# A hybrid attention and convolution layer: one signed difference block for pattern 1, and x scaled before its transposes

## The chip, the core and the metric

The kernel runs on one core of a Trainium2 chip. The metric is the device time of one execution in microseconds (us). Within a core TensorE (PE) does matmuls and transposes, VectorE (DVE), ScalarE (ACT) and GpSimd (POOL) work on elements, and SyncE (SP) issues most DMA transfers. Each engine runs its instructions in the order in which they were issued to it; what passes between engines waits on semaphores. Matmuls write into PSUM, eight banks of 128 x 512 floats; all other operands lie in SBUF.

## The reference

One layer on x of 2048 tokens by 1024 columns: a normalisation, one input projection, two groups of mixers, one output projection, a second normalisation, and the residual. There are 12 heads of 64 columns and 256 convolution columns.

```python
h = rmsnorm(x, norm_pre_g)
z = einsum('bsd,de->bse', h, w_in)                    # 1024 -> 4096 columns
q, k, v, g_attn, c_h, c_b, c_c, g_conv = split(z)
q, k = rope(q, pos), rope(k, pos)
for window, dilation in ((128, 1), (512, 4), (2048, 16)):
    # query i sees keys i, i - dilation, ..., i - window, by softmax
    o_i, lse_i = dilated_window_attn(q, k, v, window, dilation)
mix_w = softmax(stack(lses), axis=0)
o = sum(mix_w[..., None] * stack(outs), axis=0)
attn_out = o * silu(g_attn)
conv_out = c_b * causal_depthwise_conv(c_c * c_h, conv_w) * silu(g_conv)
y = einsum('bse,ed->bsd', concatenate([attn_out, conv_out]), w_out)
x = x + rmsnorm(y, norm_post_g)
```

A key at distance 128 from its query belongs to all three patterns. Mixing the three outputs by the softmax of their log-sums is the same as one softmax in which a key counts as often as patterns hold it.

## The kernel before

**Number format.** Every float operand of a product is split into a high part (rounded to fp32r) and a low part (the rest), and a product is three matmuls: high by high, high by low, low by high. ScalarE writes most high parts, VectorE most low parts, by a subtraction that reads the high part.

**Tiling.** The tokens are four chunks b of 512. The 4096 columns are eight groups; groups 0 and 7 are convolution (`conv_unit`), 1 to 6 are pairs of heads (`attn_unit`, index p). So there are 32 steps n = 4 * group + b, 24 of them attention units. A step projects a chunk onto its group's 512 columns: 4 column blocks x 8 pieces kt of 128 rows of x x 3 = 96 matmuls of 512 columns (L961 to L963).

**The first chunks.** `x_chunk(b)` loads four tiles of 128 tokens, transposes them by 128-column pieces kt (TensorE, L504), scales each transposed piece by the weights g of the normalisation while splitting it (ScalarE L511 the high part, VectorE L513 the low part), and stores it to `xt_d` in DRAM, from which the groups 1 to 7 read it again. Beside this it squares the rows (L519), finds the factors 1/RMS (`rsqrt_mean`, twelve small VectorE operations, L429 to L435), and TensorE spreads them over partitions (L526), so that they can multiply the columns: the table t holds cosine, sine (both times the factor) and the factor. Products of q and k are scaled with the rotation, V, the gate and the convolution by the third part of the table (L546, L635).

**One attention unit.** Scores (TensorE, L711 for the patterns of dilation 4 and 16, which are handled together as kind 4, L739 for pattern 1) go to PSUM with 64 rows in use; VectorE adds a mask and takes the row's extreme (L718, L746), ScalarE makes the exponentials P (L722, L750). A key that kind 4 holds twice has ln 2 in its mask. In pattern 1 each block of 128 queries has two blocks of keys, the previous one and its own; P of a query block is 128 x 256. `parts` transposes up to four 128 x 128 blocks of P into one bank (L779), ScalarE copies the high parts (L784) and VectorE takes the low parts (L785) into a tile `pt` (three of them), and `times` multiplies them by V: 256 columns, high and low side by side (L811); where one key block serves two query blocks of pattern 1, one matmul of 512 columns does both (L801). V holds its own high and low parts in 64 columns each, so that the result's bank has four quarters, of which three are wanted. `gather` joins them for each half of 256 queries: ScalarE copies two quarters into two tiles a and t (L827, L828), VectorE adds the third to a (L829), and GpSimd adds a and t (L869). The weights of the two kinds come from their sums (L885 to L909) by way of DRAM, multiply the two results (L918, L919), and GpSimd adds them and applies the gate (L920, L921).

**Output.** When all 32 steps are done, the output projection runs in a form with seven products in place of eight (L1129 to L1131); `finish` and `store` square its rows, take 1/RMS (`rsqrt_root`, L440 to L443), add the residual (L1164) and store (L1166).

**What sets the order.** No order is written out. Each operation is recorded by `add` with an engine, an estimated duration, a priority and what it reads and writes. `Plan.shift` adds the entries of the table SHIFT to the priorities (key: a hundred of priorities and a place in the code). `Plan.schedule` plays a list scheduler over the recorded operations with the program's own cost functions (`actt`, `dvet`, `poolt`, `mmt`, `dmat`) and takes the first ready operation by priority for a free engine; `mode` 1 marks score matmuls (going in or out costs 0.22 in the plan) and `mode` 2 transposes; `port=True` says that VectorE and GpSimd are not planned at once. Banks (`st`, eight of them) and buffers are rings that the plan hands out. `emit` then issues the instructions in the order of the planned starts. So any change of an estimate, or of the operations, moves others.

## Time and profile before

| | |
|---|---|
| median of 3 runs | 1181.58 us (1181.55 to 1181.8) |
| the profiled execution, its own time | 1181.31 us |
| its span in the trace | 1179.3 us |
| mean granted TensorE clock | 0.998 of full speed |
| first and last start of the transposes of P (L779) | 144.2 and 966.0 us |
| VectorE's largest group, L785 | 115.8 us of 180 instructions |
| bytes moved | 280.44 MB, mean 238 GB/s |

The span is shorter than the execution's time by 2.0 us, which lie before its first and behind its last instruction. A group's row in the profile gives the line, the engine, the operation, out <- in by the program's names, the count, busy us, mean ns of one, and the idle time of the engine just before these instructions with what ended it. In a timeline row the first two numbers are start and length in us. Ends of matmuls are modelled, and neighbours overlap in the records.

### The profile page before, as it was taken

Reading aid. Unit: us, or ns where it says so; the run is one execution under the profiler, and the core shown is the slowest. Engines: PE = TensorE matmul, PEld = TensorE weight load, DVE = VectorE, ACT = ScalarE, POOL = GpSimd, SP = SyncE. Lnnn points to the kernel's source line nnn. Section 1 sums busy time; section 2 is a strip of 40 time slices with the busy share of each in tenths; the row PEclk is TensorE's granted clock in tenths of the full one; section 3 lists DMA queues with packets and bytes.
Section 4 is the critical chain, followed back from the end, with each engine's and each line's share of the span. In section 5 each row is a group of like instructions: output and inputs, shape, how many; then the busy total and the mean of one; then the engine's idle time right before and its main releaser. Section 6 shows DMA issues by size and latency. Waiting matters only on the chain.

```text
span 1179.3 us, 20614 instructions
## 1 busy us (share of the span) xinstructions
PE 1167.9 (99%) x6620; PEld 980.1 (83%) x6620; DVE 932.6 (79%) x2331; ACT 707.2 (60%) x1875; POOL 268.5 (23%) x212
## 2 busy tenths in 40 slices
PE   8999999999999999999999999999999999999997
PEld 7888888888888888888888888888888788888886
DVE  4566467886778977897888968898888889788886
ACT  6452356776666776675677658666766653454443
POOL 0001122323223233223332322233322313100000
PEclk9999999999999999999999999999999999999999
DMA  9989867777688856788677676677766878645452
GB/s 333 365 341 349 273 226 234 233 213 240 180 253 264 267 185 206 213 280 272 218 235 237 208 238 219 226 263 252 238 187 215 324 247 334 202 141 189 138 182 89
DMA packets 175292, 280.44 MB, mean 238 GB/s; under 512 B 53712, under 2 KB 109776, under 8 KB 175184
## 3 DMA queue, kind: packets, MB, share of 16 engines
q1 hardware_dynamic: 174896, 278.86, 71.7%
q8 instruction: 52, 0.85, 0.3%
q14 instruction: 56, 0.46, 0.1%
q10 hardware_dynamic: 288, 0.27, 0.1%
HBM read 215.42 MB, written 51.05 MB: 226 GB/s over the span
## 4 chain that ended last, share of the span: by engine, by line
PE 93%; DVE 3%; DMA 2%; ACT 1%; issue 0%; SPq 0%; DVEq 0%; ACTq 0%
PE st L961 19%; PE st L963 19%; PE st L962 19%; PE st L779 6%; PE st L811 6%; PE st L1131 4%; PE st L1130 4%; PE st L1129 4%; PE st L711 4%; PE st L739 3%; PE st L801 2%; PE st L504 1%; PE st L675 1%; DMA xt<-xt 1%; DMA g<-in_w_in 0%; DMA p<-in_x 0%
## 5 line engine op out<-in xcount | busy, mean ns | idle before, releaser
L961 PE MATMUL st<-xt,w 128*128 128x512 f32 x1024 | 414.3, 405 | 0.0
L963 PE MATMUL st<-xt,w 128*128 128x512 f32 x1024 | 400.8, 391 | 0.7 <-DVE w L471 0.7
L962 PE MATMUL st<-xt,w 128*128 128x512 f32 x1024 | 399.7, 390 | 0.1
L963 PEld LDWEIGHTS st<-xt,w 128*128 128x128 f32 x1024 | 192.2, 188 | 43.9 <-DVE w L471 1.5
L961 PEld LDWEIGHTS st<-xt,w 128*128 128x128 f32 x1024 | 192.5, 188 | 40.8 <-issue 5.9
L962 PEld LDWEIGHTS st<-xt,w 128*128 128x128 f32 x1024 | 193.0, 188 | 33.1 <-DVE xt L513 0.4
L722 ACT ACTIVATE p<-p,sm 128x128 f32<-128x128 f32 (+3 forms) x192 | 105.8, 553 | 73.6 <-DVE sm L718 73.5
L785 DVE TENSOR_TENSOR pt<-st,pt 128x512 fp32r<-128x512 f32 (+1 forms) x180 | 115.8, 675 | 24.0 <-ACT pt L784 22.7
L827 ACT COPY uu<-st 64x256 f32<-64x256 f32 x192 | 69.6, 366 | 94.2 <-PE st L811 86.4
L829 DVE TENSOR_TENSOR uu<-st,uu 64x256 f32<-64x256 f32 x192 | 78.8, 419 | 57.8 <-ACT uu L828 49.4
L718 DVE CUSTOM_DVE_ANT_0 p<-st,cst 128x128 f32<-128x128 f32 (+3 forms) x192 | 82.0, 486 | 40.8 <-PE st L711 40.4
L811 PE MATMUL st<-pt,v 128*128 128x256 f32 x660 | 111.7, 284 | 0.2 <-DVE pt L785 0.2
L811 PEld LDWEIGHTS st<-pt,v 128*128 128x128 f32 x660 | 98.9, 189 | 9.4 <-DVE pt L785 0.9
L869 POOL TENSOR_TENSOR uu<-uu 128x512 f32<-128x512 f32 x48 | 69.5, 1449 | 155.1 <-DVE uu L829 113.4
L784 ACT CAST pt<-st 128x512 fp32r<-128x512 f32 (+1 forms) x180 | 96.7, 579 | 8.9 <-PE st L779 7.8
L750 ACT ACTIVATE p<-p,e 128x256 f32<-128x256 f32 (+1 forms) x192 | 94.4, 496 | 3.4 <-DVE e L746 3.3
L779 PE MATMUL st<-cst,p 128*128 128x128 f32 x708 | 95.1, 273 | 0.0
L779 PEld LDWEIGHTS st<-cst,p 128*128 128x128 f32 x708 | 82.2, 140 | 11.0 <-issue 0.9
L920 POOL TENSOR_TENSOR uu<-uu 128x512 f32<-128x512 f32 x24 | 37.3, 1556 | 170.1 <-DVE uu L919 170.1
L828 ACT COPY uu<-st 64x256 f32<-64x256 f32 x192 | 68.5, 367 | 10.6 <-POOL uu L921 5.6
L643 POOL TENSOR_TENSOR rp<-rp,cs 128x512 f32<-128x512 f32 x24 | 37.8, 1573 | 142.4 <-DMA rp<-rp 115.7
L746 DVE CUSTOM_DVE_ANT_0 p<-st,cst 128x256 f32<-128x256 f32 (+1 forms) x192 | 66.7, 411 | 3.5 <-PE st L739 3.4
(240 smaller groups left out, 1885.4 us busy)
## 6 DMA issues: line engine op xcount, KB each, us to landing
xt<-xt SPq DMA_DIRECT2D x256, 512.0 KB
cs<-t SPq DMA_DIRECT2D x28, 768.0 KB
raw<-in_w_in SPq DMA_DIRECT2D x58, 256.0 KB
rp<-rp SPq DMA_DIRECT2D x192, 64.0 KB
vd<-v SPq DMA_DIRECT2D x24, 512.0 KB
v<-vd SPq DMA_DIRECT2D x96, 128.0 KB
ab<-ad SPq DMA_DIRECT2D x48, 256.0 KB
uu<-mix SPq DMA_DIRECT2D x27, 256.0 KB
```

The costliest lines, as they stand in the source:

```text
L718: add("DVE", dvet(w) + 0.01, pr + URG, lambda h=h, r=r, P4=P4: vec.tensor_tensor_reduce(P4.ap[:, r, 0:w], ps[h].ap[:, (r - r0) * w:(r - r0 ...
L722: add("ACT", actt(w) + 0.19, pr, lambda h=h, r=r, P4=P4: act.activation(P4.ap[:, r, 0:w], P4.ap[:, r, 0:w], AF.Exp, bias=s4(0, h)[:, r:r + ...
L750: add("ACT", actt(256 - lo[g]) + 0.19, pr, lambda h=h, g=g, P1=P1: act.activation(P1.ap[:, g, lo[g]:], P1.ap[:, g, lo[g]:], AF.Exp, bias=E ...
L779: nc.tensor.transpose(ps.ap[:, i * 128:(i + 1) * 128], pp.ap[:, a, c * 128:(c + 1) * 128], ident)
L784: add("ACT", actt(m * 128, True), pr + URG, lambda: act.copy(pt.ap[:, :m, 0, :], p4()), r=[ps], w=[(pt, 0)])
L785: add("DVE", dvet(m * 128), pr + URG, lambda: vec.tensor_tensor(pt.ap[:, :m, 1, :], p4(), f(pt.ap[:, :m, 0, :]), op=ALU.subtract), r=[ps, ...
L811: mm(dst, v, pt.ap[:, i], start=s, stop=e, skip_group_check=kind == 1)
L827: add("ACT", actt(256, True) + HALF / 2, pr + URG, lambda: act.copy(cols(a, lo), o()[hi:hi + 64, 0]), r=[O], w=[(a, (h, half))])
L829: add("DVE", dvet(256), pr + URG, lambda: vec.tensor_tensor(cols(a, lo), o()[lo:lo + 64, 0], cols(a, lo), op=ALU.add), r=[O], w=[(a, (h, h ...
L961: mm(z.ap, w.ap[:, 0, js], xt.ap[:, 0], start=kt == 0, stop=False)
L962: mm(z.ap, w.ap[:, 0, js], xt.ap[:, 1], start=False, stop=False)
L963: mm(z.ap, w.ap[:, 1, js], xt.ap[:, 0], start=False, stop=kt == KT - 1)
```

## The change

**Pattern 1.** The mask of the previous block now keeps only keys nearer than 128, so that of the two blocks of a query block, previous and own, at most one has an entry at each place. The key at distance 128 is counted three times in kind 4 instead (ln 3 in its mask). `square` subtracts the previous block from the own one in SBUF (VectorE, L859) and transposes the difference: four transposes into one bank per head (L866). The positive part is the own block, the negative part the previous one. ScalarE takes each by a Relu with scale 1 or -1 (L873), VectorE the low parts by a max or min with 0 and a subtraction or addition (L880, L876), with the sign turned, so that `gather` subtracts where it added. No matmul of 512 columns is left in PV (L898).

**Joining.** ScalarE copies one quarter (L914); VectorE adds the second and adds or subtracts the third (L919, L917). The tile t and GpSimd's addition go.

**x.** For chunks 1 to 3 the rows are squared early, and x is multiplied in place by the factors (ScalarE rows 0 and 2, L541; VectorE rows 1 and 3, L538) before it is transposed (L552). For these chunks nothing is spread over partitions, the table holds cosine and sine alone and is read from the input, the gate's tanh reads PSUM directly (L591, L592), and V and the convolution's columns are copied by ScalarE (L700, L638, L596). Chunk 0 is scaled by its table as before (L570, earlier L526).

**Start and end.** The first loads of x and weights go out earlier and by two queues; the first tile of x is transposed into two banks, one scaled by ScalarE and one by VectorE (`first_tile`); the 12 matmuls of its piece run as four high by high, four high by low, four low by high; the warm-up has 7 products, not 8, and two later ones go. `rsqrt_root` has one operation less on the chain, and the last output tile is stored in two halves, the second through ScalarE's queue.

**The plan.** Some estimates change (GpSimd's constant 0.25 to 0.07, those of the weights' small operations, the cost of going into transposes 0.07 to 0.02), and the table SHIFT has other entries throughout.

```diff
-    prev1 = np.where(tk >= tq, zero, no)
+    prev1 = np.where(tk > tq, zero, no)
...
-    prev4 = np.where(four, np.where(k >= q, twice, zero), near)
-    diag4 = np.where(k <= q, np.where(four, twice, zero), no)
+    thrice = np.float32(-np.log(3.0))
+    prev4 = np.where(four, np.where(k >= q, np.where(k - q == 96, thrice, twice), zero), near)
+    diag4 = np.where(k <= q, np.where(four, np.where(q - k == 32, thrice, twice), zero), no)
...
 SHIFT = {
-    (-1, 41): 100, (0, 15): 90, (1, 8): 3, (1, 41): 120, (4, 63): 90, (4, 72): 60, (4, 76): 240, (5, 64): 203,
+    (-2, 27): -10, (0, 13): -123, (0, 29): -90, (1, 13): 260, (1, 14): -220, (1, 16): -150, (1, 45): 120,
...
-                        o.dur += 0.07
+                        o.dur += 0.02
...
-    return n * 0.00239 + 0.25
+    return n * 0.00239 + 0.07
...
-        vec.tensor_scalar(t, t, -0.5, 1.5, op0=ALU.mult, op1=ALU.add)
-        vec.tensor_tensor(y, y, t, op=ALU.mult)
+        vec.scalar_tensor_tensor(y, t, 1.5, y, op0=ALU.add, op1=ALU.mult)
...
+        if b:
+            factors(b * 100 - 150)
+            for i, z in enumerate(xn):
+                if i % 2:
+                    x_last.append(add("DVE", dvet(D), b * 100 - 140, lambda i=i, z=z: vec.tensor_scalar(
+                        z.ap, z.ap, root.ap[:, 8 + i:9 + i], None, op0=ALU.mult), r=[root], w=[(z, h) for h in range(5)], port=True))
+                else:
+                    x_last.append(add("ACT", actt(D, ptr=True), b * 100 - 140, lambda i=i, z=z: act.activation(
+                        z.ap, z.ap, AF.Copy, scale=root.ap[:, 8 + i:9 + i]), r=[root], w=[(z, h) for h in range(5)]))
...
+        def square(h):
+            pp, ps, first = P[h, 1], Tok(st_r), int(b == 0)
+            add("DVE", dvet(C), pr, lambda: vec.tensor_tensor(
+                pp.ap[:, first:, 128:], pp.ap[:, first:, 128:], pp.ap[:, first:, 0:128], op=ALU.subtract),
...
+                for g in range(4):
+                    nc.tensor.transpose(ps.ap[:, g * 128:(g + 1) * 128], pp.ap[:, g, 128:], ident)
...
+            for s, pt in enumerate(two):
+                lo = first if not s else 0
+                add("ACT", actt((4 - lo) * 128, True), pr + URG, lambda pt=pt, lo=lo, s=s: act.activation(
+                    pt.ap[:, lo:, 0, :], p4(lo), AF.Relu, scale=1.0 if s else -1.0), r=[ps], w=[(pt, 0)])
+                if s:
+                    add("DVE", dvet(C), pr + URG, lambda pt=pt: vec.scalar_tensor_tensor(
+                        pt.ap[:, :, 1, :], p4(0), 0.0, f(pt.ap[:, :, 0, :]), op0=ALU.max, op1=ALU.subtract, reverse1=True),
...
-            add("ACT", actt(256, True) + HALF / 2, pr + URG, lambda: act.copy(cols(t, lo), o()[lo:lo + 64, 1]), r=[O], w=[(t, (h, half))])
...
+            for l in range(2):
+                if l and kind == 1:
+                    fn = lambda: vec.tensor_tensor(cols(a, lo), cols(a, lo), o()[lo:lo + 64, 1], op=ALU.subtract)
+                else:
+                    fn = lambda l=l: vec.tensor_tensor(cols(a, lo), o()[lo:lo + 64, l], cols(a, lo), op=ALU.add)
...
-                    add("POOL", poolt(C), pr, lambda a=a, t=t: pool.tensor_tensor(a.ap, a.ap, t.ap, op=ALU.add), r=[t], w=[a], port=True)
...
-    add("PE", 3.4, -1e6, lambda: warm_up(8), w=[warm])
+    add("PE", 3.0, -1e6, lambda: warm_up(7), w=[warm])
```

Three places show what the new plan does with it. In the rows below out <- in are the program's names with the number of the buffer, then the shape.

The first is TensorE in the first stage, where chunk 0's projections end (L961 to L963 before, L1062 to L1064 after), its factors are spread (L526, L570) and chunk 1's transposes begin (L504, L552). Before:

```order
L961 MATMUL st_117<-xt_127,w_136 128x512
L962 MATMUL st_117<-xt_127,w_136 128x512
L963 MATMUL st_117<-xt_127,w_136 128x512
L526 MATMUL st_115<-cst,sm_161 128x128 x4
L961 MATMUL st_118<-xt_127,w_136 128x512
L962 MATMUL st_118<-xt_127,w_136 128x512
L963 MATMUL st_118<-xt_127,w_136 128x512
```

After:

```order
L1062 MATMUL st_117<-xt_126,w_135 128x512
L1063 MATMUL st_117<-xt_126,w_135 128x512
L1064 MATMUL st_117<-xt_126,w_135 128x512
L570 MATMUL st_112<-cst,sm_158 128x128 x4
L552 MATMUL st_118<-cst,p_185 128x128
L552 MATMUL st_118<-cst,p_186 128x128
L552 MATMUL st_118<-cst,uu 128x128 x2
L552 MATMUL st_111<-cst,p_185 128x128
L552 MATMUL st_111<-cst,p_186 128x128
```

Before, 63 of the step's 96 matmuls stood ahead of the spread, 33 behind it, and chunk 1's transposes began 21 matmuls later. Now all 96 stand ahead of it, and the transposes of chunk 1's eight pieces follow in a row.

The second is TensorE in the middle of an attention unit, at pattern 1 of one head. Before, the end of one head's PV (L801, L811) and the transposes of the next blocks:

```order
L811 MATMUL st_117<-pt_193,v_179 128x2x128
L801 MATMUL st_117<-pt_193,v_177 128x2x2x128
L811 MATMUL st_117<-pt_193,v_177 128x2x128
L779 MATMUL st_116<-cst,p_188 128x128 x4
L779 MATMUL st_114<-cst,p_189 128x128 x4
L779 MATMUL st_115<-cst,p_189 128x128 x4
L961 MATMUL st_119<-xt_126,w_133 128x512
L962 MATMUL st_119<-xt_126,w_133 128x512
```

After, at one head's square (L866):

```order
L898 MATMUL st_114<-pt_188,v_174 128x2x128
L898 MATMUL st_114<-pt_189,v_174 128x2x128
L1062 MATMUL st_116<-xt_123,w_132 128x512
L1063 MATMUL st_116<-xt_123,w_132 128x512
L1064 MATMUL st_116<-xt_123,w_132 128x512
L866 MATMUL st_113<-cst,p_186 128x128 x4
L1062 MATMUL st_112<-xt_124,w_133 128x512
L1063 MATMUL st_112<-xt_124,w_133 128x512
L1064 MATMUL st_112<-xt_124,w_133 128x512
```

Groups of four transposes, two of them for each head, have become one; 18 projection matmuls stand between this one and the eight PV matmuls that need its two tiles.

The third is VectorE at the same place. Before, the low parts (L785) with the additions of the joining (L829) and one of q's splits (L659):

```order
L785 TENSOR_TENSOR pt_193<-st_116,pt_193 128x4x128
L785 TENSOR_TENSOR pt_191<-st_115,pt_191 128x4x128
L659 TENSOR_TENSOR q_170<-rp_142,q_170 128x512
L785 TENSOR_TENSOR pt_192<-st_121,pt_192 128x4x128
L829 TENSOR_TENSOR uu<-st_118,uu 64x256
L829 TENSOR_TENSOR uu<-st_114,uu 64x256
L918 TENSOR_TENSOR uu<-uu,ab_159 128x512
```

After, the two splits of that square (L880, L876) with the joining (L919, L917), the weights' products (L1007, L1008) and a rotation (L710):

```order
L1007 TENSOR_TENSOR uu<-uu,ab_156 128x512
L1008 TENSOR_TENSOR uu<-uu,ab_156 128x512
L919 TENSOR_TENSOR uu<-st_117,uu 64x256
L917 TENSOR_TENSOR uu<-uu,st_117 64x256
L919 TENSOR_TENSOR uu<-st_114,uu 64x256
L917 TENSOR_TENSOR uu<-uu,st_114 64x256
L710 TENSOR_TENSOR rp_141<-rp_141,cs_191 128x512
L880 SCALAR_TENSOR_TENSOR pt_190<-st_113,pt_190 128x4x128
L876 SCALAR_TENSOR_TENSOR pt_188<-st_113,pt_188 128x4x128
```

Each half of the joining has become a pair, and the two splits of a square read one bank, st_113, and stand behind two such pairs and a rotation.

More of the change, by code (lines that the diff above doesn't have):

```diff
@@ L461, in weights_in @@
             else:
-                add("ACT", 0.45, -2e6, lambda: nc.scalar.dma_start(raw.ap, w_in[i, :, grp, :]), w=[raw], land=4.0)
+                add("DMA", dmat(256), -1.995e6, lambda: nc.sync.dma_start(raw.ap, w_in[i, :, grp, :]), w=[raw], land=3.6)
         else:
@@ L516, in x_chunk @@
             add("DMA", dmat(512), max(p2, -50) + 60, lambda kt=kt, s=s: nc.sync.dma_start(xt_d[b][kt], f(s.ap)), r=[s], w=[("xt", b, kt)])
-        pr = b * 100 - 40
-        for i, z in enumerate(xn):
-            x_last.append(add("ACT", actt(D), pr + i, lambda i=i, z=z: act.activation(junk, z.ap, AF.Square, accum_out=root.ap[:, i:i + 1]),
-                              r=[z], w=[(root, i), "junk"], after=XL[3:4]))
+        if b:
+            return
+        pr = -40
+        factors(pr)
         pr += 8
-        add("DVE", 2.6, pr, lambda: rsqrt_mean(root.ap), w=[root])
         def spread():
@@ L589, in tap @@
             return u.ap[:, j:j + 4].rearrange("p r i -> p (r i)")
-        add("DVE", dvet(C), pe, lambda: vec.tensor_tensor(bb.ap, zs[2].ap, t.ap[:, 2], op=ALU.mult), r=[zs[2], (t, 2)], w=[bb])
-        g = silu2(zs[3], t, pe, natural, placed)
+        taken(zs[2], bb)
+        g = silu2(zs[3], True if b else t, pe, natural, placed)
         y = Tok(rp_r)
@@ L787, in parts, with tr, p4 @@
             return {ac: (pt, i) for i, ac in enumerate(blk)}
+        def square(h):
+            pp, ps, first = P[h, 1], Tok(st_r), int(b == 0)
+            add("DVE", dvet(C), pr, lambda: vec.tensor_tensor(
+                pp.ap[:, first:, 128:], pp.ap[:, first:, 128:], pp.ap[:, first:, 0:128], op=ALU.subtract),
+                r=[(pp, g) for g in range(first)] , w=[(pp, g) for g in range(first, 4)], port=True)
+            two = Tok(pt_r), Tok(pt_r)
+            def tr():
+                for g in range(4):
+                    nc.tensor.transpose(ps.ap[:, g * 128:(g + 1) * 128], pp.ap[:, g, 128:], ident)
+            add("PE", 0.436, pr, tr, r=[(pp, g) for g in range(4)] + ["cst"], w=[ps] + [(pt, "hold") for pt in two], mode=2)
+            def p4(lo):
+                return ps.ap[:, lo * 128:].rearrange("p (i c) -> p i c", c=128)
+            for s, pt in enumerate(two):
[5 more added lines that the diff above has]
+                        pt.ap[:, :, 1, :], p4(0), 0.0, f(pt.ap[:, :, 0, :]), op0=ALU.max, op1=ALU.subtract, reverse1=True),
+                        r=[ps, (pt, 0)], w=[(pt, 1)])
+                else:
+                    add("DVE", dvet((4 - lo) * 128), pr + URG, lambda pt=pt, lo=lo: vec.scalar_tensor_tensor(
+                        pt.ap[:, lo:, 1, :], p4(lo), 0.0, f(pt.ap[:, lo:, 0, :]), op0=ALU.min, op1=ALU.add),
+                        r=[ps, (pt, 0)], w=[(pt, 1)])
+            return {(g, s): (two[s], g) for g in range(4) for s in range(2) if not (b == 0 and g == 0 and s == 0)}
         def times(h, kind, where, O):
-            pairs = [ac for ac in where if kind == 1 and ac[1] == 1 and ac[0] % 2 == 0 and (ac[0] + 1, 0) in where
-                     and where[ac[0] + 1, 0] == (where[ac][0], where[ac][1] + 1)]
             def pv():
@@ L844, in attn_unit @@
                     bl = [(r, j) for r in range(4) for j in range(b + 1)]
-                else:
-                    bl = [(g, s) for g in range(4) for s in range(2) if not (b == 0 and g == 0 and s == 0)]
                 if h == 0:
-                    UU[kind] = Tok(uu_r), Tok(uu_r)
+                    UU[kind] = Tok(uu_r)
                 O = [Tok(st_r), Tok(st_r)]
@@ L864, in attn_unit @@
                                 times(h, kind, part, O[half])
+                else:
+                    where = square(h)
+                    for half in range(2):
+                        times(h, 1, {ac: v for ac, v in where.items() if ac[0] // 2 == half}, O[half])
                 for half in range(2):
                     gather(h, kind, half, O[half])
-                if h == 1:
-                    a, t = UU[kind]
-                    add("POOL", poolt(C), pr, lambda a=a, t=t: pool.tensor_tensor(a.ap, a.ap, t.ap, op=ALU.add), r=[t], w=[a], port=True)
         X = Tok(ex_r)
@@ L956, in hybrid_layer, with proj @@
               xt, w = XT[n, kt], W[grp, kt] if conv else W[grp, j // 2, kt // 2]
+              if n == kt == 0:
+                if j == 0:
+                    for l, m in ((0, 0), (0, 1), (1, 0)):
+                        def proj(l=l, m=m, xt=xt, w=w, zs=zs):
+                            for k in range(4):
+                                mm(zs[k].ap, w.ap[:, l, k * 128:(k + 1) * 128], xt.ap[:, m], start=l == m, stop=False)
+                        done = add("PE", 4 * mmt(C), 50 + 0.01 * (2 * l + m), proj, r=[(w, l), (xt, 2 * m), (xt, 2 * m + 1)], w=zs)
+                        later = x_last[2 if l or m else 1]
+                        later.deps.add(done)
+                        done.outs.append(later)
+                        later.wait += 1
+                continue
               def proj(j=j, kt=kt, xt=xt, w=w, z=zs[j], conv=conv):
```

161 lines of the change are left out of this document (107 added, 54 removed), and 17 rows, old and new, of the table SHIFT.

## The prediction

> **What bounds the kernel now.** I read the page's first part, then who TensorE waited for, then one window over the attention stages.
>
> ```profile
> span 1179.3 us, 20614 instructions
> PE 1167.9 (99%) x6620; PEld 980.1 (83%) x6620; DVE 932.6 (79%) x2331; ACT 707.2 (60%) x1875; POOL 268.5 (23%) x212
> PE 93%; DVE 3%; DMA 2%; ACT 1%; issue 0%; SPq 0%; DVEq 0%; ACTq 0%
> ```
>
> ```profile
> PE st L526 <- DVE sm L435: 1.7, 1, 1.7
> ...
> PE st L963 <- DVE w L471: 0.7, 1, 0.7
> ...
> PE st L811 <- DVE pt L785: 0.2, 1, 0.2
> ```
>
> ```profile
> 144.00:966.00 822.00, 821.15 (x4990) 692.37 (x4988) 673.75 (x1788) 552.30 (x1560) 238.04 (x187) 1.00 0.74 235
> ```
>
> TensorE is 99% busy, and its chain is 93% of the span. Its longest wait is 1.7 us, and between 144 and 966 us it waits for 0.9 us (0.7 and 0.2). So an instruction taken off its queue there is worth its whole slot, as long as nothing else becomes late. The window's columns after the length are TensorE, its weight loads, VectorE, ScalarE and GpSimd: VectorE is next, at 673.75 of 822 us, or 82%. The profiled execution took 1181.3 us (its span and 2.0 us around it), 0.3 us below the median of 1181.58 us; I sum against 1181.3 and add 0.3.
>
> **Transposes taken away.** Pattern 1 had eight transposes per head (seven in the first chunk): 18 x 2 x 8 + 6 x 2 x 7 = 372. With one difference block per query block there are four: 24 x 2 x 4 = 192. So 180 go, and of the 16 that spread the RMS factors 12 go.
>
> ```profile
> 705.62 1.04 PE L779 MATMUL st<-cst,p 128*128 128x128 f32 x8
> ...
> 706.73 0.39 PE L962 MATMUL st<-xt,w 128*128 128x512 f32 x1
> 706.95 0.39 PE L963 MATMUL st<-xt,w 128*128 128x512 f32 x1
> ```
>
> The first column is the start, and ends are modelled, so I count from start to start. From the first of eight transposes to the second matmul behind them are 1.11 us; a matmul of 512 columns takes 0.23, so the eight cost 0.88, or 0.109 us each, with the return to matmuls in it. 192 x 0.109 = **-20.9 us**.
>
> **PV matmuls cut apart.** The 96 joined ones of 512 columns become 192 of 256.
>
> ```profile
> 154.45 0.40 PE L801 MATMUL st<-pt,v 128*128 128x512 f32 x1
> 154.68 0.40 PE L811 MATMUL st<-pt,v 128*128 128x256 f32 x2
> 154.92 0.39 PE L801 MATMUL st<-pt,v 128*128 128x512 f32 x1
> ```
>
> A joined one takes 0.23 us and two single ones 0.24: **+0.5 us** (bounds 0 and 1).
>
> **Score matmuls in more pieces.** These use 64 rows, and going in and out of them costs. The new order has 53 unbroken runs of them where the old had 43.
>
> ```profile
> 248.56 1.75 PE L739 MATMUL st<-kk,q 64*128 64x256 f32 x24
> 250.25 0.66 PE L779 MATMUL st<-cst,p 128*128 128x128 f32 x4
> ```
>
> ```profile
> 452.39 0.40 PE L963 MATMUL st<-xt,w 128*128 128x512 f32 x1
> 452.72 1.07 PE L739 MATMUL st<-kk,q 64*128 64x256 f32 x12
> 453.73 0.66 PE L779 MATMUL st<-cst,p 128*128 128x128 f32 x4
> ```
>
> 24 in one run take 1.69 us, 12 take 1.01: cut in two, the 24 would take 2.02, 0.33 more. The matmul ahead of a run gives up 0.33 instead of 0.23, so a run can cost 0.4 or 0.5; beside transposes it costs less. 10 x 0.35 = **+3.5 us** (bounds 2 and 5).
>
> **The start.** Three waits are touched.
>
> ```profile
> 4.94 1.55 PE L504 MATMUL st<-cst,p 128*128 128x128 f32 x8 [0.31 <-DMA p<-in_x]
> 6.70 0.48 PE L961 MATMUL st<-xt,w 128*128 128x512 f32 x1
> 7.24 0.50 PE L962 MATMUL st<-xt,w 128*128 128x512 f32 x1
> ...
> 24.88 0.39 PE L963 MATMUL st<-xt,w 128*128 128x512 f32 x1
> 26.98 0.65 PE L526 MATMUL st<-cst,sm 128*128 128x128 f32 x4 [1.72 <-DVE sm L435]
> ```
>
> Now x's two first pieces go out first, on two queues, and four transposes, not eight, stand ahead of the first product: about 0.4 us. Its lo half has four hi products to hide behind: the 0.3 us between 6.70 and 7.24 goes. The spread of the factors moves behind all 96 matmuls of chunk 0, 33 of them later than before (33 x 0.23 = 7.6 us), so its 1.9 us go, and 0.5 with the bank wait: 3.1 in all. What is late next is new: chunk 1's rows must be squared, their factors found and the rows scaled before a transpose may start.
>
> ```profile
> 22.21 1.06 ACT L519 ACTIVATE ab<-p 128x1024 f32<-128x1024 f32 x1
> ...
> 23.40 1.06 ACT L519 ACTIVATE ab<-p 128x1024 f32<-128x1024 f32 x1
> ...
> 24.58 0.17 DVE L429 TENSOR_SCALAR sm<-sm 128x4 f32<-128x4 f32 x1 [0.60 <-ACT ab L519]
> ```
>
> Chunk 0's squares end at 24.58, where the factors' first operation starts; four more at 1.19 (22.21 to 23.40) make 29.3, the factors 2.4 (24.58 to 26.98, where the spread follows) 31.7, and two scalings on ScalarE beside two on VectorE some 2.2 (two squares' time): 33.9. TensorE would be there at about 32 (24.88 and the 7.6). Chunk 1's loads stand ahead of four stores in SP's queue now and can land earlier, so 33.9 is the late end: a wait of 0 to 2 us. All eight of the chunk's tiles are then transposed in a row and compete for eight banks: 0.5 more. I take **-1.5 us** (bounds -3 and +1). Scaling x spares nothing on TensorE later.
>
> **The end.** One small operation of four goes from the last factor's chain, and the last output leaves in two halves by two queues.
>
> ```profile
> 1174.43 0.15 DVE L442 TENSOR_SCALAR ys<-ys 128x1 f32<-128x1 f32 x1
> 1174.62 0.16 DVE L443 TENSOR_TENSOR ys<-ys 128x1 f32<-128x1 f32 x1
> ...
> 1175.59 0.99 SPq L1166 DMA_DIRECT2D out<-raw  x2
> ```
>
> 0.2 for the operation and 0.3 of the 0.5 that SP's second issue takes: **-0.5 us** (0 to -0.8).
>
> **VectorE, the cover.** It is given the subtraction of the two blocks (48, in SBUF), one more addition per half and head (96), and 96 splits by min or max in place of 96 plain ones; it loses, in the window, 18 gate and 18 V scalings.
>
> ```profile
> L785 DVE TENSOR_TENSOR pt<-st,pt 128x512 fp32r<-128x512 f32 x168 | 109.8, 684 | 23.5 <-ACT pt L784 22.3
> L829 DVE TENSOR_TENSOR uu<-st,uu 64x256 f32<-64x256 f32 x192 | 78.8, 419 | 57.8 <-ACT uu L828 49.4 <-ACT uu L827 5.3 <-PE st L963 0.7
> L546 DVE TENSOR_TENSOR g<-st,cs 128x512 f32<-128x512 f32 x32 | 24.9, 780 | 0.1
> L513 DVE SCALAR_TENSOR_TENSOR xt<-st,gp,xt 128x512 fp32r<-128x512 f32 x32 | 22.6, 743 | 25.8 <-ACT xt L511 25.8
> ```
>
> 48 x 0.684 + 96 x 0.419 + 96 x (0.743 - 0.684) - 18 x 0.78 - 18 x 0.684 = 32.8 + 40.2 + 5.7 - 14.0 - 12.3 = +52.4 us. In the window that is 726 of some 805 us, 90% for 82%. ScalarE, at 552.30 in the window, loses half of its copies for the joining. GpSimd loses its 48 additions of 1.45 us, which helps VectorE:
>
> ```profile
> L869 POOL TENSOR_TENSOR uu<-uu 128x512 f32<-128x512 f32 x48 | 69.5, 1449 | 155.1 <-DVE uu L829 113.4 <-ACT uu L828 26.8 <-DMA xt<-xt 7.7
> L784 ACT CAST pt<-st 128x512 fp32r<-128x512 f32 x168 | 91.6, 586 | 8.0 <-PE st L779 7.0
> ```
>
> ```profile
> 397.10 1.76 POOL L643 TENSOR_TENSOR rp<-rp,cs 128x512 f32<-128x512 f32 x1
> 397.62 2.39 DVE L643 TENSOR_TENSOR rp<-rp,cs 128x512 f32<-128x512 f32 x2
> ...
> 401.25 0.69 DVE L643 TENSOR_TENSOR rp<-rp,cs 128x512 f32<-128x512 f32 x1
> ```
>
> Beside GpSimd's multiplication one of VectorE's takes 1.2 us (two in 2.39), alone 0.69. The Trainium skill, GPSIMD Engine Reference, section 1 (Specifications), says that GpSimd's SBUF interfaces are shared with VectorE and contend with its instructions that have two SBUF inputs. The trace agrees; by that rule the new subtraction, which has two, is exposed to it, and the splits out of PSUM are not.
>
> A PV matmul waits for both splits. Free of queueing, the chain behind the last transpose is one ScalarE evacuation (0.59, L784's), two splits (1.49) and hand-overs (about 0.3): 2.4 us. The order puts at least 15 matmuls of 512 or their like between, 3.4 us, and 18 at the place shown (4.1). So a square has 1.0 us of slack before TensorE waits. I cost what breaks through at **+1.5 us** (from 0 to the first rival), as 0.9 broke through before with 8 points more idle time.
>
> **Sum:** -20.9 + 0.5 + 3.5 - 1.5 - 0.5 + 1.5 = -17.4; 1181.3 - 17.4 + 0.3 = **1164 us**. With the terms' ends it lies between 1159 and 1169.
>
> **Rivals.**
> 1. *VectorE is late at the squares*, 0.15 to 0.25 us each on average: 48 of them make 7 to 12 us in place of 1.5, so 1170 to 1175. For it: 90% busy in strict order, and at the place shown two addition pairs (1.7 us) and a rotation stand ahead of the splits. Against: these belong to work that is ready earlier, and GpSimd lets go of it. Chance 0.22.
> 2. *The start goes wrong*: scaling makes chunk 1 late by 4 us or more beyond the sum, 1167 to 1169. For it: everything there waits for the squares; against: loads stand earlier. The clock is a second way:
>
> ```profile
> 1.11 3.51 PE L933 MATMUL st<-pa 128*128 128x128 f32 x16 [1.11 <-DVE u L573]
> ...
> 6.33 0.61 PE L933 MATMUL st<-pa 128*128 128x128 f32 x4
> ```
>
> Warm-up matmuls step by 0.21 us at first and by 0.11 at 6.33, so the clock doubles within the warm-up; two instructions of the 16 go, and 7 x 2 x 0.21 = 3.0 us remain. Were the doubling missed for as long again, 3.4 us of work would take twice that: +1.7 to 3.4 us, 1166 to 1167. The Trainium skill, TensorE: Matmul & The Clock Gate, Part 1, has the full clock released after a busy window of about 3.4 us which runs freely and does not start with the kernel; by that rule the shorter warm-up could just miss it. Chance of both 0.07.
> 3. *Slower*: each square's PV matmuls come over 0.36 us late (17.4 / 48), as when a rotation beside GpSimd (1.2 us) and two additions (0.8) stand ahead of the splits as a rule: 2.0 against 1.0 of slack, 0.45 late after what the queue absorbs, 48 x 0.45 = 21.6 in place of 1.5: 1184. Only at such a rate does it decide; the trace has a single wait of a PV matmul for an evacuation (L785), 0.2 us long. Chance 0.05.
> 4. *It does not do what it says*: the slots freed are filled by waits that the transposes had hidden, 1178 to 1183. The 0.9 us of waits speak against it. Chance 0.03.
>
> **How the numbers follow.** The forecast has 0.63, on 1159 to 1169. With the second rival that is 0.70; half of the first is needed for 8 in 10, so the range goes to 1173. Under about 0.2% (2.4 us) this kernel can't be told from no change. Forecast and rivals 1 and 2 are faster by more: 0.92; the fourth is within: 0.03; the third slower: 0.05.
>
> **What would show it.** In the profile after: transposes of pattern 1 at 192 and still 0.109 us a slot; TensorE busy about 1150 us; VectorE near 90% in the window, 970 in all; the factor wait gone from TensorE's list, and a wait of the first chunk-1 transpose for a scaling of 0 to 2 us. A list of TensorE's waits for pattern 1's splits above 5 us would prove the first rival; score runs that cost under 0.2 us each, or a start that gains 4 us, would put the time below 1160.

## The result, and the profile after

The changed kernel takes 1167.51 us (median of 4 runs, 1166.8 to 1169.19), the kernel before 1181.69 us: a ratio of 0.9881, 95% interval 0.9864 to 0.9898. A later set of runs gave 1172.42 us (1167.23 to 1173.99), a ratio of 0.9914 (0.9885 to 0.9942). So the change gains 9.5 to 14.2 us; the forecast was 17.4, its range 1159 to 1173. The kernel before stayed within 1180.7 and 1183.3 in every set; the changed one scatters over 7 us, which is part of the story below.

The profile's first part and its chain, of the changed kernel (its slowest execution of the first set, 1169.19 us):

```profile
span 1166.8 us, 20226 instructions
PE 1154.8 (99%) x6518; PEld 964.2 (83%) x6518; DVE 980.4 (84%) x2523; ACT 668.0 (57%) x1722; POOL 187.3 (16%) x158
PE 88%; DVE 6%; ACT 2%; DMA 2%; issue 1%; SPq 1%; DVEq 0%; ACTq 0%
```

The span is 12.5 us shorter. TensorE still looks 99% busy, but its share of the chain fell from 93 to 88%, and VectorE's rose from 3 to 6%: the path to the end now goes through VectorE at some places. The window over the attention stages (length, then TensorE, weight loads, VectorE, ScalarE, GpSimd) and TensorE's list of waits (total, times, longest) say how much:

```profile
144.00:954.00 810.00, 806.91 (x4895) 675.58 (x4894) 733.53 (x1982) 495.54 (x1382) 166.45 (x140) 1.00 0.75 231
```

```profile
PE st L898 <- DVE pt L876: 1.5, 2, 1.2
...
PE st L898 <- ACT rp L591: 1.1, 1, 1.1
PE st L1051 <- ACT xt L494: 0.7, 1, 0.7
PE st L898 <- issue: 0.3, 1, 0.3
```

TensorE is idle for 3.1 of 810 us in the attention stages, where it was 0.9 of 822, and VectorE is at 733.5 of 810 us, 91%. The waits named are of PV matmuls (L898) for pattern 1's low parts (L876). The one put down to L591 is of this kind too: it ends at 836.8 us, where the splits were done at 836.63 and L591, a tanh of the gate, 0.03 us later.

The list names too little, so I summed all of TensorE's time from start to start, by what the instruction is. The last two columns are experiments in the same order, told below:

| TensorE's time, us | before | after | after, again | double_T | pool_short |
|---|---|---|---|---|---|
| projections | 724.0 | 726.9 | 727.8 | 722.6 | 722.7 |
| PV | 102.5 | 104.4 | 104.4 | 102.6 | 102.6 |
| scores | 92.8 | 95.6 | 95.9 | 95.2 | 94.5 |
| transposes | 95.3 | 75.8 | 76.3 | 97.3 | 76.1 |
| output projection | 152.1 | 152.2 | 152.2 | 152.2 | 152.2 |
| warm-up, ahead of the first, behind the last start | 12.6 | 12.0 | 11.8 | 11.8 | 11.4 |
| span | 1179.3 | 1166.8 | 1168.4 | 1181.5 | 1159.5 |

A wait counts in the row of the instruction ahead of it. The transposes lost 19.5 us, near what they should; scores, PV and projections together gained 7.6. Ten more runs of score matmuls are part of that; the two columns at the right, in which no wait for pattern 1 is left, show that most of it is waiting.

One of the two long waits shows how they arise. VectorE, ScalarE, GpSimd and TensorE around 699 us, from the timeline of the changed kernel (start, length, engine, line; in brackets the idle time before, with its releaser):

```profile
695.44 0.69 DVE L710 TENSOR_TENSOR rp<-rp,cs 128x512 f32<-128x512 f32 x1
696.16 1.67 DVE L714 TENSOR_TENSOR rp<-rp,rp 128x512 f32<-128x512 f32 x1
697.75 0.41 DVE L919 TENSOR_TENSOR uu<-st,uu 64x256 f32<-64x256 f32 x1
698.20 0.41 DVE L917 TENSOR_TENSOR uu<-uu,st 64x256 f32<-64x256 f32 x1
698.53 0.41 DVE L919 TENSOR_TENSOR uu<-st,uu 64x256 f32<-64x256 f32 x1
698.98 0.41 DVE L917 TENSOR_TENSOR uu<-uu,st 64x256 f32<-64x256 f32 x1
699.52 0.56 DVE L880 SCALAR_TENSOR_TENSOR pt<-st,pt 128x384 fp32r<-128x384 f32 x1
700.00 0.68 DVE L876 SCALAR_TENSOR_TENSOR pt<-st,pt 128x512 fp32r<-128x512 f32 x1
```

```profile
697.87 0.62 ACT L720 CAST kk<-rp 128x512 fp32r<-128x512 f32 x1 [2.43 <-DVE rp L714]
698.51 0.98 ACT L873 ACTIVATE pt<-st 128x384 fp32r<-128x384 f32 x2
```

```profile
695.57 1.71 POOL L710 TENSOR_TENSOR rp<-rp,cs 128x512 f32<-128x512 f32 x1 [24.39 <-ACT uu L914]
697.24 1.75 POOL L1009 TENSOR_TENSOR uu<-uu 128x512 f32<-128x512 f32 x1
```

```profile
695.56 0.60 PE L866 MATMUL st<-cst,p 128*128 128x128 f32 x4
...
700.83 1.07 PE L898 MATMUL st<-pt,v 128*128 128x256 f32 x7 [1.23 <-DVE pt L876]
```

The square's transposes are done by 696.0. But VectorE's last step of K's rotation (L714) takes 1.67 us in place of the 0.69 that it takes where GpSimd's work beside it is cut (pool_short, below), and two queues carry the delay to the splits. In VectorE's own, two pairs of the joining (L919, L917) stand between the rotation and the splits, so that these could not start before 699.4. In ScalarE's, the cast of K (L720) waits for the rotation and stands ahead of the two Relus (L873), which start at 698.5 and are done at 699.0 and 699.5; that holds the first split back by 0.1 us more. The splits end at 700.7, and PV comes 1.2 us late. At 835 us it is the same rotation step (1.66 us); there ScalarE's cast holds up a copy of the joining (L914), and VectorE idles 0.48 us for it.

How the rotation is slowed can be read from the starts. In the first trace 27 of VectorE's 192 rotations, splits of q and k and products by the weights start while one of GpSimd's additions or multiplications runs; they take 1.66 us in the median, and 24 of them end 0.54 to 0.55 us after GpSimd's instruction does. Another 18 were already running when one of GpSimd's started, and took no more than 0.69. So one of VectorE's that starts second is held until GpSimd's is done, and a tenth of a microsecond decides. In the first trace one multiplication (L710) starts at 695.44, ahead of GpSimd's at 695.57; in the second it comes behind and costs 1.1 us more:

```profile
695.67 1.77 DVE L710 TENSOR_TENSOR rp<-rp,cs 128x512 f32<-128x512 f32 x1
```

```profile
695.55 1.35 POOL L710 TENSOR_TENSOR rp<-rp,cs 128x512 f32<-128x512 f32 x1 [24.63 <-DMA rp<-rp]
```

### The profile page after: what moved, and what is told of

It reads as the page before. It is cut to its first block, busy times and chain, and to the rows that moved or that the text cites. A ratio compares the mean times of both kernels' runs of the same rounds, so it can differ in the third digit from the quotient of the medians.

```text
span 1166.8 us, 20226 instructions
## 1 busy us (share of the span) xinstructions
PE 1154.8 (99%) x6518; PEld 964.2 (83%) x6518; DVE 980.4 (84%) x2523; ACT 668.0 (57%) x1722; POOL 187.3 (16%) x158
## 4 chain that ended last, share of the span: by engine, by line
PE 88%; DVE 6%; ACT 2%; DMA 2%; issue 1%; SPq 1%; DVEq 0%; ACTq 0%
PE st L1062 18%; PE st L1064 17%; PE st L1063 17%; PE st L898 8%; PE st L1230 4%; PE st L1231 4%; PE st L1232 4%; PE st L778 4%; PE st L806 3%; PE st L846 3%; PE st L866 2%; PE st L552 1%; DVE uu L919 1%; DVE rp L710 1%; PE st L742 1%
## 5 line engine op out<-in xcount | busy, mean ns | idle before, releaser
L1062 PE MATMUL st<-xt,w 128*128 128x512 f32 x1020 | 414.0, 406 | 0.0
L1064 PE MATMUL st<-xt,w 128*128 128x512 f32 x1020 | 399.1, 391 | 0.0
L1064 PEld LDWEIGHTS st<-xt,w 128*128 128x128 f32 x1020 | 191.5, 188 | 42.4
L1062 PEld LDWEIGHTS st<-xt,w 128*128 128x128 f32 x1020 | 192.0, 188 | 39.2 <-issue 6.4
L919 DVE TENSOR_TENSOR uu<-st,uu 64x256 f32<-64x256 f32 x288 | 118.8, 419 | 25.8 <-ACT uu L914 20.6
L898 PEld LDWEIGHTS st<-pt,v 128*128 128x128 f32 x852 | 116.0, 190 | 13.9 <-ACT rp L700 1.6
L898 PE MATMUL st<-pt,v 128*128 128x256 f32 x852 | 121.9, 284 | 2.8 <-DVE pt L876 1.5
L914 ACT COPY uu<-st 64x256 f32<-64x256 f32 x192 | 67.7, 367 | 90.5 <-PE st L898 83.9
L1009 POOL TENSOR_TENSOR uu<-uu 128x512 f32<-128x512 f32 x24 | 35.1, 1462 | 455.3 <-DVE uu L1008 403.1
L785 DVE CUSTOM_DVE_ANT_0 p<-st,cst 128x128 f32<-128x128 f32 (+3 forms) x192 | 82.1, 484 | 8.6 <-PE st L778 8.4
L710 DVE TENSOR_TENSOR rp<-rp,cs 128x512 f32<-128x512 f32 x72 | 58.8, 835 | 17.3 <-DMA rp<-rp 17.3
L852 DVE TENSOR_TENSOR pt<-st,pt 128x512 fp32r<-128x512 f32 x84 | 55.6, 684 | 6.7 <-ACT pt L851 6.1
L873 ACT ACTIVATE pt<-st 128x512 fp32r<-128x512 f32 (+1 forms) x96 | 50.9, 583 | 15.5 <-PE st L866 14.4
L778 PE MATMUL st<-kk,q 64*128 64x128 f32 (+3 forms) x576 | 55.8, 332 | 0.2 <-DVE g L592 0.2
L720 ACT CAST kk<-rp 128x512 fp32r<-128x512 f32 x24 | 14.9, 622 | 71.4 <-DVE rp L714 71.4
L778 PEld LDWEIGHTS st<-kk,q 64*128 64x128 f32 x576 | 42.4, 185 | 13.8 <-issue 6.7
L851 ACT CAST pt<-st 128x512 fp32r<-128x512 f32 x84 | 46.6, 581 | 8.6 <-PE st L846 7.8
```

The costliest lines, as they stand in the source:

```text
L710: add(e, dur, pr, lambda o=o, a=a, i=i, eng=eng: eng.tensor_tensor(o.ap, a.ap, cs.ap[:, i], op=ALU.mult), r=[cs], w=[o], port=True)
L778: mm(ps[h].ap[:, (r - r0) * w:(r - r0 + 1) * w], Q.ap[lo:lo + 64, i, r * 128:(r + 1) * 128], KK[j][lo:lo + 64, 4 * r:4 * r + 4, 0:w // 4]. ...
L785: add("DVE", dvet(w) + 0.01, pr + URG, lambda h=h, r=r, P4=P4: vec.tensor_tensor_reduce(P4.ap[:, r, 0:w], ps[h].ap[:, (r - r0) * w:(r - r0 ...
L898: mm(dst, v, pt.ap[:, i], start=s, stop=e, skip_group_check=False)
L914: add("ACT", actt(256, True) + 0.09, pr + URG, lambda: act.copy(cols(a, lo), o()[hi:hi + 64, 0]), r=[O], w=[(a, (h, half))])
L919: fn = lambda l=l: vec.tensor_tensor(cols(a, lo), o()[lo:lo + 64, l], cols(a, lo), op=ALU.add)
```

## The experiments

Each kernel changes one thing; "in its own order" means that the plan is the changed kernel's, instruction for instruction, so that only durations differ. Where an edit makes the plan order anew, the entries of SHIFT are kept at the operations that they had.

**The changed kernel again** (no edit).

> The changed kernel once more, unaltered. Theory A (order and port decide): the long waits of TensorE for pattern 1's splits, 1.4 us at 699 us and 1.2 us at 835 us of the first trace, come again at the same two places, since every engine's order and VectorE's slow rotations beside GpSimd are fixed; time 1167 to 1169 us. Theory B (arrival of transfers decides, and varies): they are elsewhere or gone, waits after 30 us lie anywhere between 2 and 5 us in all, and the time varies by as much: 1166.5 to 1169.5 us.

1172.42 us (1167.23 to 1173.99), above what either theory gave. The waits came at the same places, 699 us (2.5 us beyond the usual step now, 1.4 in the first trace) and 837 us (1.2), so theory A holds for the places; the amount varies more than I had expected, by the order of starts shown above. The runs beside the profile reach 1174.

**A filled gap in the warm-up.** In `first_tile`, behind the second pair of transposes:

```diff
+                if h:
+                    warm_up(3)
```

> Three more warm-up products stand behind the first tile's four transposes, where TensorE stood idle for about 1 us; all else keeps its place. Clock theory: the first four products took 0.46 us each and the next eight 0.30, because the idle time let the clock stay low; with the gap filled the doubling comes by about 6.5 us, the twelve products of the first tile end about 1.4 us earlier (the 13th product starts near 10.6 us, not 12.0), and the time is 1166.1 us for 1167.5. Rival: the doubling does not depend on the gap, the extra products only push the first product by up to 0.3 us, and the time is 1167.5 to 1167.8.

1168.31 us (1165.05 to 1169.62), overlapping the unaltered kernel's runs on the same chip. The rows below are both without the filler, of the changed kernel's first trace and of its second:

```profile
6.22 2.05 PE L1051 MATMUL st<-xt,w 128*128 128x512 f32 x4 [0.67 <-ACT xt L494]
8.07 1.05 PE L552 MATMUL st<-cst,p 128*128 128x128 f32 x4
```

```profile
6.07 1.20 PE L1051 MATMUL st<-xt,w 128*128 128x512 f32 x4 [1.05 <-DVE xt L498]
7.11 0.60 PE L552 MATMUL st<-cst,p 128*128 128x128 f32 x4
...
10.10 0.44 PE L552 MATMUL st<-cst,p 128*128 128x128 f32 x2 [0.55 <-DMA p<-in_x]
11.02 0.87 PE L552 MATMUL st<-cst,p 128*128 128x128 f32 x6 [0.48 <-DMA p<-in_x]
```

The same program took four products in 1.85 us (6.22 to 8.07) or in 1.04 (6.07 to 7.11): the clock doubles later in one execution than in another, with the gap in both. And it hardly matters, since the next transposes wait for x to arrive: the 13th product starts at 12.0 us in the first trace, 11.65 in the second, 11.63 with the filler. My clock theory, by which the 13th would start near 10.6 with the gap filled, fell; the start is bound mostly by x's transfers.

**Transposes twice**, in the order of the changed kernel:

```diff
-                for g in range(4):
+                for g in (0, 1, 2, 3, 0, 1, 2, 3):
```

> Each of the 192 transposes of the difference blocks is issued twice into the same bank, in the unchanged order: TensorE has as many transposes again as the change took away. Theory (TensorE bounds, 0.109 us a slot): +20.9 us, less the 1.7 to 3 us of waits for VectorE that the extra time covers: 1185.5 to 1187 us. Rival (the freed slots are filled by waits, another engine bounds): the extra transposes fall into idle time and cost under 12 us, below 1180.

1184.16 us (1183.33 to 1185.58), 1.3 us under the theory's range and above the rival's 1180. As a difference it lies at the rival's bound of 12: 11.7 us more than the changed kernel on the same chip, 16.7 more than in its first set. The table has the reason: the transposes take 97.3 us for 76.3, 20.9 more, 0.109 for each of 192; but projections and PV take 7 us less. The waits are gone, since a later TensorE finds its operands ready: its list holds nothing for pattern 1. So the transposes are worth 20.9 us on TensorE, and 6 to 9 of them came back as waits.

**More score runs.** `VISIT = 2` becomes 1.

> The plan may open a visit of score matmuls with fewer free banks: 78 unbroken runs of score matmuls in place of 53, the same instructions otherwise (140 runs of transposes for 136). Theory: a run costs TensorE 0.46 us by the trace of the changed kernel (entry, exit and the slower steps beside it): 25 x 0.46 = +11.5 us, 1179 us, and 0.35 as I had predicted would give 1176. Rival: the runs cost nothing by themselves and what moved was waiting: the time stays within 3 us of 1167.5, unless the waits named by the profile grow.

1183.57 us, 11.2 more than the changed kernel on the same chip: 0.45 us for each of 25 runs. From start to start the score matmuls themselves take 6.2 us more (102.1 for 95.9), the matmuls just ahead of and behind a run 0.09 and 0.11 more each; the rest of the 14.9 us between the two spans are waits and, behind one of 2.1 us, a stretch of 3.4 us at half clock. So a run costs about 0.45, more than the 0.35 that I had taken; this is an estimate, since the scores' own row has waits in it too.

**GpSimd cut short.** Its rotation of q and its last two operations of a unit work on 16 of 512 columns, in the order of the changed kernel:

```diff
-            lambda o=o, a=a, i=i, eng=eng: eng.tensor_tensor(o.ap, a.ap, cs.ap[:, i], op=ALU.mult),
+            lambda o=o, a=a, i=i, eng=eng, n=C if e == "DVE" else 16: eng.tensor_tensor(
+                o.ap[:, 0:n], a.ap[:, 0:n], cs.ap[:, i, 0:n], op=ALU.mult),
...
```

> The changed kernel in its own order, but GpSimd's rotation of q and its two last operations of each attention unit work on 16 columns in place of 512 (left out: the other 496). Theory (VectorE is late because its operations in SBUF take 1.2 us and more beside GpSimd's): the two long waits at 699 and 836 us go, TensorE's waits of the attention stages fall from 5.5 us to under 1.5, the time is 1161 to 1164 us and the runs lie within 2 us of each other. Rival (VectorE simply has too much to do in this order, whatever GpSimd does): the waits stay, 1167 to 1172.

1162.89 us (1161.61 to 1163.77), with no wait for pattern 1 left. The groups of VectorE's rotation (busy us, mean ns, idle before), first in the changed kernel, then here:

```profile
L710 DVE TENSOR_TENSOR rp<-rp,cs 128x512 f32<-128x512 f32 x72 | 58.8, 835 | 17.3 <-DMA rp<-rp 17.3
L714 DVE TENSOR_TENSOR rp<-rp,rp 128x512 f32<-128x512 f32 x24 | 21.4, 893 | 0.7
```

```profile
L710 DVE TENSOR_TENSOR rp<-rp,cs 128x512 f32<-128x512 f32 x72 | 47.9, 684 | 15.6 <-DMA rp<-rp 15.6
L714 DVE TENSOR_TENSOR rp<-rp,rp 128x512 f32<-128x512 f32 x24 | 16.6, 692 | 0.7
```

With GpSimd cut short beside them the same instructions take 0.68 and 0.69 us. VectorE's busy time falls by 31 us (949.5 for 980.4), the span to 1159.5 us, and the table shows where: 4 us of projections, 2 of PV, 1 of scores. One of the 4 is none of GpSimd's: the first tile's twelve products take 3.3 us here and 4.3 in the changed kernel's first trace, where the clock doubled later. The theory holds for the two long waits, whose rows show the slowed rotation. For the smaller ones it is likely but not shown, since GpSimd's own results come earlier here too. The runs lie within 2.2 us of each other, where the unaltered kernel's span 7.

**No subtraction.** Two of 128 columns of each difference block, in the order of the changed kernel:

```diff
-                pp.ap[:, first:, 128:], pp.ap[:, first:, 128:], pp.ap[:, first:, 0:128], op=ALU.subtract),
+                pp.ap[:, first:, 128:130], pp.ap[:, first:, 128:130], pp.ap[:, first:, 0:2], op=ALU.subtract),
```

> The changed kernel in its own order, but the subtraction of the two blocks works on 2 columns of 128 for each query block (left out: the other 126), which takes about 48 x 0.55 = 26 us from VectorE. Theory (slowed rotations decide): the waits at 699 and 836 us stand behind a rotation and not behind a subtraction, so they shrink but stay; time 1164 to 1168. Rival (VectorE's load decides): the waits go, 1161 to 1163.

1170.31 us (1169.81 to 1171.34), above the theory's range: taking 22 us of busy time from VectorE (958.2) does not bring the time below the changed kernel's own, and the wait at 700 us is there (2.5 us). At the second place 0.5 us is left of 1.2. The rival is refuted. What I had not expected is in the windows behind that wait (TensorE's busy time is the second number, the granted clock the last but two):

```profile
696.00:700.00 4.00, 4.00 (x21) 3.18 (x19) 3.93 (x5) 0.50 (x2) 3.92 (x3) 1.00 0.49 109
700.00:703.40 3.40, 1.10 (x9) 0.90 (x8) 3.23 (x7) 1.89 (x5) 1.03 (x2) 1.00 1.03 372
703.40:706.90 3.50, 3.50 (x13) 2.81 (x12) 3.10 (x7) 1.59 (x4) 1.93 (x2) 0.51 1.04 407
706.90:712.00 5.10, 5.10 (x42) 4.20 (x43) 3.26 (x16) 0.94 (x3) 0.62 (x1) 1.00 0.89 313
```

After 2.3 us without work the clock is at half for 3.5 us, which costs at least another 1.3 us: seven matmuls there step by 0.4 in place of 0.23. So a long wait can be paid for one and a half times. It need not be: in the changed kernel's second trace TensorE also stands without work for 2.3 us, from 699.85 to 702.13, and the clock stays at 1.00 behind it.

**The square alone**, in the kernel before (`square`, the masks, GpSimd subtracting for pattern 1, and the changed estimates for GpSimd and the weights' operations):

```diff
+                elif kind == 1:
+                    where = square(h)
+                    for half in range(2):
+                        times(h, 1, {ac: v for ac, v in where.items() if ac[0] // 2 == half}, O[half])
...
```

> The kernel before with the difference block of pattern 1 alone (x, the joining by ScalarE, VectorE and GpSimd, start and end as before; GpSimd's estimate and those of the weights' small operations as changed; the table's entries stay at their operations). TensorE does 180 transposes less, 96 joined matmuls cut, and has 54 runs of score matmuls for 43. Theory: -19.6 + 0.9 + 11 x 0.46 = -13.6 and waits of 3 to 8 us more, since VectorE gains 33 us of subtractions and GpSimd keeps its additions: 1171 to 1176 for 1181.9. Rival (the other two parts carry the gain: without them VectorE's port is crowded and eats it): 1178 to 1184.

1194.8 us: slower than the kernel before by 13 us, outside of what either theory gave. TensorE's own saving is there (transposes 77.7 us for 95.3), but its list of waits is long:

```profile
PE st L676 <- DVE rp L636: 3.0, 4, 1.5
PE st L841 <- DVE pt L814: 3.0, 4, 1.3
PE st L841 <- DVE pt L810: 2.3, 8, 0.4
PE st L841 <- DVE pt L786: 1.8, 6, 0.5
```

**The square undone**, in the changed kernel (`parts` with the old grouping in place of `square`, all parts added).

> The changed kernel with pattern 1's blocks transposed one by one again (180 transposes more, no subtraction, plain low parts; single PV matmuls and the new joining stay, entries of the table stay at their operations). Runs of score matmuls: 48 for 53. Theory: +19.6 - 5 x 0.46 = +17.3, less 4 to 6 us of waits that VectorE's lighter load and TensorE's longer stream cover: from 1167.5 to 1172 for the changed kernel, 1179 to 1183. Rival (the transposes' slots were already filled by waits): 1172 to 1176.

1186.62 us (1185.44 to 1187.37): 14 to 19 us slower than the changed kernel, above the theory's range, and 5 us slower than the kernel before, although the other two parts are in.

**The joining undone**, in the changed kernel:

```diff
-            for l in range(2):
-                ...
+            add("ACT", actt(256, True) + 0.09, pr + URG, lambda: act.copy(cols(t, lo), o()[lo:lo + 64, 1]), ...)
+            add("DVE", dvet(256), pr + URG, lambda: vec.tensor_tensor(cols(a, lo), o()[lo:lo + 64, 0], cols(a, lo), op=ALU.add), ...)
...
+                    add("POOL", poolt(C), pr, lambda a=a, t=t, kind=kind: pool.tensor_tensor(
+                        a.ap, a.ap, t.ap, op=ALU.subtract if kind == 1 else ALU.add), r=[t], w=[a], port=True)
```

> The changed kernel with the joining of before: ScalarE copies two quarters, VectorE adds one, GpSimd adds (or, for pattern 1, subtracts) the second tile. VectorE loses 96 operations of 0.42 us (40 us), GpSimd gets 48 of 1.45 us back (70 us). Runs of score matmuls: 58 for 53 (+2.3 us). Theory (VectorE is late because of what GpSimd does beside it): the waits for the low parts grow, 1173 to 1181 us. Rival (VectorE's own load decides): with 40 us less to do its waits shrink, 1164 to 1169.

1183.04 us (1180.85 to 1186.97). VectorE has 43 us less to do (937.0) and GpSimd 76 more, and the kernel is 11 to 16 us slower: the direction of the theory and more, against the rival.

**x unscaled**, in the changed kernel (factors spread and tables scaled for all chunks, V, gate and convolution scaled by VectorE).

> The changed kernel with x of chunks 1 to 3 unscaled as before: the factors are spread by 12 more transposes (1.3 us), V, gate and convolution columns are scaled by the table on VectorE (54 operations of some 0.7 us more there, ScalarE's copies go), the tables hold three parts and go through DRAM. 54 runs of score matmuls for 53. Theory: +1.8 us by TensorE's own work, and waits of 3 to 10 us more, since VectorE's queue is longer ahead of pattern 1's low parts: 1172 to 1180. Rival (scaling x brings nothing beyond its 12 transposes, as I had put it): 1168 to 1173.

1193.81 us, far above both. These four kernels all lose more than their operations explain, which asked for the next two.

**The changed kernel and the kernel before without their tables** (`SHIFT = {}`).

> The changed kernel with an empty table SHIFT: all operations the same, only their order is the plan's own; 55 runs of score matmuls and 141 of transposes for 53 and 136. Theory: the table keeps VectorE's queue clear ahead of the waits, and is worth 5 to 10 us: 1173 to 1179. Rival (the order hardly matters, the operations do): 1167 to 1172.

> The kernel before with an empty table SHIFT: the same operations in the plan's own order; 47 runs of score matmuls and 152 of transposes for 43 and 129. It is compared with the changed kernel without its table (1181.2 us). Theory A (the operations carry the gain, a table of its own is worth the same 9 to 14 us to either kernel): 1191 to 1196 us. Theory B (the new table carries it: in the plan's own order the two kernels stand equal): 1180 to 1185 us.

1181.18 us (1180.13 to 1182.77) and 1190.33 us (1189.88 to 1190.92): the first above its theory's range, the second 0.7 us under theory A's and far from B's. With not one operation changed, losing its table costs the changed kernel 8.8 to 13.7 us, and the kernel before 8.4 (1181.89 beside it). Between the two without tables the change is worth 9.2 us. So the operations carry 9 us in the plan's own order too, and the table that came with the change adds up to 5 more than the old one did for the old kernel (0.3, by the second set). It also follows that the four kernels above, whose tables were made for other operations, cannot price the parts: their order alone may cost them as much.

## Why the prediction was right, and by how much

**Transposes, -20.9.** Right: 0.109 us each in double_T to the third digit. The table's row fell by 19.5: those of P by 20.6 and the spread by 1.3, while those of x and V gained 2.4.

**PV cut apart, +0.5.** 102.5 to 102.6 us where no waits lie in it (pool_short): +0.1.

**Scores, +3.5.** In the two columns without such waits the scores take 1.7 and 2.4 us more than before; beside the runs there are 4 more matmuls ahead at 0.09, 2 more behind at 0.11 and 14 more borders with transposes and PV at 0.06 to 0.1, some 1.7 us: 3.4 to 4.1 in all. By the price of visit1, ten runs would be 4.5. Right within its bounds, and rather low.

**Start, -1.5.** When the sixth step's projections begin (131.9 us, before 134.0), the change stands at -2.1, -2.4 and -2.8 us in the three traces of this start (first, second, double_T); 1.3 of it are the twelve spread transposes, so the start is worth 0.8 to 1.5. The wait for the factors is gone, and chunk 1's transposes did not wait for their scaling (they start at 33.4, behind the spread). The first tile brought nothing: the 13th product starts at 12.0 and 11.7 us, before at 10.7. In the second trace TensorE waits 1.0 us there for x's later pieces.

**End, -0.5.** Nothing: from the last matmul's start to the end are 7.3 us before, 7.5 after, 7.2 in pool_short. The operation less on the chain is there, but the second half goes out last, by ScalarE's queue:

```profile
1162.67 0.81 SPq L1274 DMA_DIRECT2D out<-cs  x2
```

```profile
1163.46 0.36 ACTq L1274 DMA_DIRECT2D out<-cs  x1
```

**New waits, +1.5.** This is the term that was mis-sized. Without waits the sum was -18.9, a span of 1160.4; pool_short, the same order without them, has 1159.5. With them it is 1166.8 and 1168.4 in the two traces (TensorE busy 1154.8 for the 1150 that I had named, 1150.2 in pool_short): 7 to 9 us, of which 0.5 to 0.8 fall into the start and 0.4 behind the last matmul. The sum's upper end, 1169, had left this term at 1.5, though its bound was the first rival. It came out at the size of that rival (7 to 12 us), and by its mechanism, VectorE late at the squares. But I had seen it as 0.2 us at each of 48 squares from a queue at 90%. VectorE did come to 91% in the window, and no_sub shows that the load was not the cause of the longest wait.

Step by step beside pool_short, the two long waits make 2.6 us of it in the first trace and 3.7 in the second. At both the slowed rotation and two pairs of the joining stand ahead of the splits: what the third rival had as a rule for 48 squares cost over a microsecond at two. Two readings of mine had hidden it. I took 1.2 us for a rotation beside GpSimd by halving a row of two, 2.39; in the trace the first of them took 1.79, beside GpSimd's, and the second 0.68, so a slowed one costs half as much again as I had counted. And I counted ScalarE's evacuation as free of queueing; its queue added 0.1 us at 699 and up to 0.5 at 835. Some 2 us more come in smaller waits between 226 and 273 us. At 228 us ScalarE was not in the way, with its Relus done at 224.6: a split of K took 1.78 us beside GpSimd, and VectorE's own queue brought pattern 1's splits late. The rest, some 1.4 and 2.4 us in the two traces, is in smaller pieces that were not traced.

The Trainium skill, GPSIMD Engine Reference, section 1 (Specifications), has GpSimd contend with VectorE's instructions that read two operands from SBUF. The rotation agrees, 835 ns on average beside GpSimd and 684 where its work is cut. The splits that read PSUM keep their 0.68 us in both, as that rule has it; I had drawn from it only that the subtraction is exposed, not that what stands ahead of the splits is.

**The rivals.** Slower by 0.45 us at each square did not happen; nor was the clock of the start the price, which made 0.3 us between the changed kernel's two traces. The forecast (1164) was 3.5 us under the first median, and the second set, at 1172.4, lies where the first rival was put.

**What stays open.** How much scaling x and the new joining are worth by themselves was not settled: no kernel with one part had a table of its own. Why the second set's runs scatter up to 1174 is known in part: the trace there has 1.1 us more at 699 us, by which engine started first. The runs of 1173.46 and 1173.99 were not profiled; their mean granted clock is 0.997, that of the set's other two 0.999, which fits a drop of the clock behind a wait but does not show one.

## What to carry to other kernels

Price what leaves the bounding engine by its slot, and then follow every operand that must now come earlier through each queue that it stands in: here one slow VectorE operation reached TensorE through what stood behind it in VectorE's own order, and a little through ScalarE's. Do not halve a merged row of the timeline: a mean of 1.2 us was one of 1.79 and one of 0.68. An engine at 90% is no cause by itself; ask which of its instructions a neighbour slows, and what waits behind them. And where a table or a planner sets the order, a part that is taken out under the old table is measured with its order spoiled: take the table from both sides first.

## What was not expected of the hardware

TensorE's clock fell to half within a kernel that is 99% busy: after 2.3 us without work it stood at 0.51 for 3.5 us (no_sub, 703.4 to 706.9), though the mean over the span is 0.998. In the changed kernel's first trace the wait of 1.2 us at 699 us was not followed by it, and in its second neither was one of 2.3 us at the same place. So the length of the wait alone does not decide. The Trainium skill, TensorE: Matmul & The Clock Gate, Part 1, puts the loss of the full clock behind an idle window of about 3.4 us; here a stretch of 3.4 us with 1.1 us of work in it was enough. That bears on the scatter as well: whether the clock drops behind such a wait or not makes a difference of over a microsecond.
